# Recurrent mixer heads: key factors as a logarithm in the exponents, once per head

## The chip, the core and the metric

The kernel runs on one core of a Trainium2 chip. The metric is the device time of one execution in microseconds (us): the median of several runs. TensorE multiplies matrices, VectorE, ScalarE and GpSimd do the elementwise work, SyncE issues most DMAs. Each engine works through its own queue in order.

## What is computed

Two transformer blocks on 512 tokens of width 1024, all in float32. The second block has a mixer with two kinds of heads, and the change is in the first kind: four recurrent heads of 128 channels (HGRN2), computed in chunks. In the reference, with q, f, k, v per head:

```python
f = lbf + (1.0 - lbf) * jax.nn.sigmoid(f_logit)
k = 1.0 - f
bc = jnp.cumsum(to_chunks(jnp.log(f)), axis=3)
decay = jnp.exp(jnp.where(causal, bt[t] - bt[s], -jnp.inf))
a = jnp.einsum('bhtd,bhsd,bhtsd->bhts', qt, kt, decay)      # within a chunk
o = einsum(a, v) + (q * exp(bt)) @ state                    # and from the chunks before
```

So the weight of key s for query t is the sum over channels of q[t] k[s] exp(b[t] - b[s]), where b is the running sum of log f. The second kind are eight stick-breaking heads. The results of both, normed and joined, go through `w_out`. Around the mixers stand three feed-forward parts, the first block's attention, a memory cross attention and the norms.

## The kernel before

Every dense product is made of three passes over split operands (a high and a low part): `mm3`, lines 372 to 374. `split` (L403 on ScalarE, L404 on VectorE) makes the parts. TensorE's order is written by the program. In the mixers `weave` makes it: a planner takes chains (heads) and fills (slabs of weights against all tokens), with a model of each step's cost on VectorE ("D"), ScalarE ("A") and GpSimd ("G"). While no step of a chain is due by that model, it takes the next piece of the fills. At most three chains are active (`WIDTH`). The other engines' queues are ordered by a list scheduler that knows the dependencies and its own estimates, and that also hands out the 16 buffers of the ring "w" (`wt()`).

A recurrent head is the chain `hgrn_chain`. L1388 makes kf = 1 - f on ScalarE, L1389 log f, L1391 the running sum b on VectorE (a scan that restarts at every chunk of 64). The causal weights are then made in levels. Level 0 is the diagonal (L1460, kf against q). For the half lengths 64, 32, 16, 8, 4, 2, 1 the tokens are taken in pairs of a lower and an upper half, and for 128 and 256 over whole chunks. For each of these nine levels `exponents` or `far_exponents` fills a buffer e of 128x512: its lower halves with ref - b, its upper halves with b - ref, on GpSimd (L1417 and L1419, or L1448 and L1450). `decayed` takes the exponential on ScalarE (L1404 and L1405 for 64, L1407 for the others), multiplies the lower halves by kf (L1408) and the upper ones by q (L1409), both on VectorE. `scores` then multiplies lower by upper on TensorE (L1468 up to 64, L1481 and L1487 beyond), and L1470 puts the product into place. The exponents are prepared `LOOK` + 1 = 3 levels ahead of the scores. `prepared` (L1501 to L1505) and `first` (L1507) tell the planner what a level and a head's beginning cost.

Other lines that the text names: a stick-breaking head (`sb_head`) masks (L1556, L1559), takes an exponential and a logarithm (L1560, L1561), scans (L1564), subtracts (L1566), takes an exponential (L1567) and is transposed on TensorE (the flips, L756). The head norm is L1365 to L1367, with L1588 (`sb_tail`) or L1533 (`hgrn_tail`) behind it. `fill_part` splits finished mixer outputs into the buffers "h" and multiplies them by slabs of `w_out`, which L1631 adds up.

Of the kernel before, what the change touches and what calls it, by code (L numbers as in the profile page):

```python
# [14 lines left out]
AF = mybir.ActivationFunctionType  # L15
ALU = mybir.AluOpType
# [4 lines left out]
D = 1024  # L21
# [57 lines left out]
def STEP(pe=0.0, dve=0.0, act=0.0, ops=(), lat=0.0, free=0, need=0, back=0):  # L79

    return Step(pe, dve, act, ops, lat, free, need, back)
# [11 lines left out]
def transformer_blocks_kernel(  # L95
# [41 lines left out]
    V, A, G, T = nc.vector, nc.scalar, nc.gpsimd, nc.tensor  # L137
# [13 lines left out]
    def big(tag, bufs, dt=F32, cols=512):  # L151
        return sp.tile([P, cols], dt, tag=tag, bufs=bufs, name=nm(tag))
# [10 lines left out]
    def wt(dt=F32):  # L163
        return big("w", WBUFS, dt)
# [4 lines left out]
    def aux():  # L169
        return pb.tile([P, 512], F32, tag="b", name=nm("b"))  # L170

    def col(n=4, bufs=20):
        return sp.tile([P, n], F32, tag=f"c{n}", bufs=bufs, name=nm("c"))
# [1061 lines left out]
    tiny, eps6 = small[:, 0:1], small[:, 1:2]  # L1235
# [148 lines left out]
    def hgrn_chain(hd):  # L1384
        q, f = store["q", hd], store["f", hd]
        yield STEP()
        kf = wt()
        A.activation(kf, f, AF.Copy, scale=-1.0, bias=1.0)  # L1388
        A.activation(f, f, AF.Ln, bias=tiny)  # L1389
        b = f  # L1390
        V.tensor_tensor_scan(out=b, data0=reset, data1=f, initial=0.0, op0=ALU.mult, op1=ALU.add)  # L1391

        bc = b.rearrange("p (c t) -> p c t", t=64)
        tot = bc[:, :, 63]

        def halves(t, hl):
            v = t.rearrange("p (b u c) -> p b u c", u=2, c=hl)
            return v[:, :, 0, :], v[:, :, 1, :]

        def decayed(e, hl):  # L1400

            el, eu = halves(e, hl)
            if hl == 64:
                A.activation(el, el, AF.Exp)  # L1404
                A.activation(eu, halves(b, hl)[1], AF.Exp)  # L1405
            else:
                A.activation(e, e, AF.Exp)  # L1407
            V.tensor_tensor(el, el, halves(kf, hl)[0], op=ALU.mult)  # L1408
            V.tensor_tensor(eu, eu, halves(q, hl)[1], op=ALU.mult)  # L1409

        def exponents(hl):
            e = wt()
            el, eu = halves(e, hl)
            bl, bu = halves(b, hl)
            nb = 256 // hl
            ref = bl[:, :, hl - 1:hl].to_broadcast([P, nb, hl])
            G.tensor_tensor(el, ref, bl, op=ALU.subtract)  # L1417
            if hl != 64:
                G.tensor_tensor(eu, bu, ref, op=ALU.subtract)  # L1419
            decayed(e, hl)  # L1420
            return e

        ad = wt()

        w0, w13, w2 = [wt(F32R) for b in range(2)], [wt(F32R) for b in range(2)], wt(F32R)
        w2 = [w2[:, :256], w2[:, 256:]]

        def diagonals(t):
            return t.rearrange("p (a c) -> p a c", c=P)[:, 0:4:3]

        def far_exponents(hl):
            nch = hl // 64
            nb = 256 // hl
            lowc, upc = col(8), col(8)
            tv = tot.rearrange("p (b u c) -> p b u c", u=2, c=nch)
            lv = lowc[:, :4].rearrange("p (b c) -> p b c", c=nch)
            uv = upc[:, :4].rearrange("p (b c) -> p b c", c=nch)
            G.tensor_copy(lv[:, :, nch - 1], tv[:, :, 0, nch - 1])
            G.memset(uv[:, :, 0:1], 0.0)
            for c in range(nch - 1):  # L1440
                G.tensor_tensor(lv[:, :, nch - 2 - c], lv[:, :, nch - 1 - c],
                                tv[:, :, 0, nch - 2 - c], op=ALU.add)
                G.tensor_tensor(uv[:, :, c + 1], uv[:, :, c], tv[:, :, 1, c], op=ALU.add)
            e = wt()
            ev = e.rearrange("p (b u c t) -> p b u c t", u=2, c=nch, t=64)
            bv = b.rearrange("p (b u c t) -> p b u c t", u=2, c=nch, t=64)
            for bb in range(nb):
                G.tensor_tensor(ev[:, bb, 0], lv[:, bb].unsqueeze(2).to_broadcast([P, nch, 64]),  # L1448
                                bv[:, bb, 0], op=ALU.subtract)
                G.tensor_tensor(ev[:, bb, 1], uv[:, bb].unsqueeze(2).to_broadcast([P, nch, 64]),  # L1450
                                bv[:, bb, 1], op=ALU.add)
            decayed(e, hl)
            return e

        def scores(hl, e):
            ps = aux()
            if hl == 0:
                for gg in range(4):
                    sl = slice(gg * P, (gg + 1) * P)
                    T.matmul(ps[:, sl], kf[:, sl], q[:, sl], start=True, stop=True)  # L1460
                V.tensor_tensor(ad.rearrange("p (g t) -> p g t", g=4),
                                ps.rearrange("p (g t) -> p g t", g=4),
                                ident.unsqueeze(1).to_broadcast([P, 4, P]), op=ALU.mult)
                return 0.43
            if hl <= 64:
                for gg in range(4):
                    up = e[:, gg * P:(gg + 1) * P].rearrange("p (b u c) -> p b u c", u=2, c=hl)[:, :, 1, :]
                    T.matmul(ps[:, gg * 64:(gg + 1) * 64], e[:, gg * P:(gg + 1) * P], up,  # L1468
                             start=True, stop=True)
                V.copy_predicated(  # L1470
                    halves(ad, hl)[1],
                    masks[hl].rearrange("p (b c) -> p b c", c=hl),
                    ps[:, :256].rearrange("p (b c) -> p b c", c=hl))
                if hl == 1:
                    split(w0[0][:, :P], w0[1][:, :P], ad[:, :P])
                    split(*[diagonals(t) for t in w13], ad.rearrange("p (a c) -> p a c", c=P)[:, 1:4:2])
                    split(w2[0][:, :P], w2[1][:, :P], ad[:, 256:256 + P])
                return 0.21
            if hl == 128:
                for bb in range(2):  # L1480
                    T.matmul(ps[:, bb * P:(bb + 1) * P], e[:, bb * 256:bb * 256 + P],  # L1481
                             e[:, bb * 256 + P:bb * 256 + 256], start=True, stop=True)
                for bb, t in enumerate((w0, w2)):
                    split(t[0][:, P:256], t[1][:, P:256], ps[:, bb * P:(bb + 1) * P])
            else:
                for bb in range(2):
                    T.matmul(ps[:, bb * 256:(bb + 1) * 256], e[:, bb * P:(bb + 1) * P],  # L1487
                             e[:, 256:512], start=True, stop=True)
                split(w0[0][:, 256:], w0[1][:, 256:], ps[:, :256])
                split(w13[0][:, P:384], w13[1][:, P:384], ps[:, 256:])  # L1490
            return 0.22 if hl == 128 else 0.86

        order = (0, 64) + LEVELS + (128, 256)
        es = {0: None}

        def prepare(n):
            if n < len(order):
                hl = order[n]
                es[hl] = far_exponents(hl) if hl > 64 else exponents(hl)

        def prepared(n):  # L1501
            if n >= len(order):
                return ()
            far = order[n] > 64
            return (("G", 2.3),) * far + (("G", 0.7), ("G", 0.7)) * (not far) + (("A", 0.55), ("D", 0.7))  # L1505

        first = (("A", 0.6), ("A", 0.6), ("D", 0.6))  # L1507
        for n in range(1, LOOK + 1):
            prepare(n)
            first += prepared(n)  # L1510
        yield STEP(ops=(first,), lat=TLAT[2], need=1)
        for n, hl in enumerate(order):
            prepare(n + LOOK + 1)
            pe = scores(hl, es.pop(hl))
            after = {0: (("D", 0.6),), 1: (("D", 0.35), ("A", 0.7), ("D", 0.75)), 128: (("A", 0.32), ("D", 0.4)),
                     256: (("A", 0.55), ("D", 0.7))}.get(hl, (("D", 0.35),))
            last = n == len(order) - 1
            yield STEP(pe=pe, ops=(after, prepared(n + LOOK + 1)), lat=HLAT, need=int(not last), free=1,
                       back=0 if last else HBACK)
        store["w", hd] = w0, [t[:, :384] for t in w13], w2, [t[:, 384:] for t in w13]  # L1520
# [352 lines left out]
```

## Time and profile before

| | |
|---|---|
| median of 3 runs | 1912.51 us (1911.18 to 1912.85) |
| profiled execution | 1912.74 us, of which the span from first to last instruction is 1911.0 us |
| TensorE busy | 1881.5 us (98%) |
| VectorE busy | 1388.6 us (73%) |
| ScalarE busy | 929.8 us (49%) |
| GpSimd busy | 174.9 us (9%) |
| mixers of the second block | about 1180 to 1430 us; recurrent heads 0 and 1 from 1213, heads 2 and 3 from 1331 us |

All shares are of the span. Matmuls overlap in the pipeline, so that a busy TensorE is one that always has an instruction under way; its granted clock is given apart, as a share of 2.4 GHz. Idle time of an engine is put down to the instruction that released it last ("<-"). Idle time of an engine other than the bound costs nothing by itself.

### The profile page before, as it was taken

The page shows a single profiled execution, that of the slowest core. Times are in us where ns is not written, and L with a number is a line of the kernel's source. Part 1 is how long each engine was busy: PE and PEld are TensorE (multiplying, and loading weights), DVE is VectorE, ACT ScalarE, POOL GpSimd, SP SyncE. Part 2 cuts the span into 40 slices and gives each one's busy share as a digit, 9 for nine tenths or more (in the row PEclk, how much of TensorE's full clock was granted, in tenths as well). Part 3 has the DMA queues.
Part 4 walks back from the last instruction along what each step waited for, and adds up shares of the span by engine and source line. Part 5 has one row for each costly group of instructions (what it writes and reads, how often), then busy time and mean ns, then how long its engine had stood idle before and what let it go on. Part 6 is the DMA issues. An engine that isn't in the chain of part 4 may idle for free.

```text
span 1911.0 us, 29337 instructions
## 1 busy us (share of the span) xinstructions
PE 1881.5 (98%) x11566; PEld 1688.3 (88%) x11566; DVE 1388.6 (73%) x2217; ACT 929.8 (49%) x1537; POOL 174.9 (9%) x272
## 2 busy tenths in 40 slices
PE   8999999999999999999999999999999999999998
PEld 6899888888999998899999988888888778999997
DVE  6777635468878786777877757888976448878785
ACT  5666534364544445443434356657565344344443
POOL 2330100060000002000000010430410000000000
PEclk9999999999999999999999999999999999999999
DMA  5212224452233324423232342121343222232322
GB/s 180 67 55 68 78 66 154 166 176 89 89 111 96 120 93 162 143 67 111 90 119 99 114 160 71 63 94 39 103 152 133 77 85 82 99 111 89 111 88 89
DMA packets 164908, 198.69 MB, mean 104 GB/s; under 512 B 7745, under 2 KB 131746, under 8 KB 164770
## 3 DMA queue, kind: packets, MB, share of 16 engines
q1 hardware_dynamic: 163202, 192.10, 30.8%
q0 software_dynamic: 1280, 4.20, 0.6%
q8 instruction: 91, 1.49, 0.3%
q10 hardware_dynamic: 288, 0.52, 0.1%
q14 instruction: 47, 0.39, 0.1%
HBM read 186.30 MB, written 10.49 MB: 103 GB/s over the span
## 4 chain that ended last, share of the span: by engine, by line
PE 87%; issue 5%; DVE 3%; ACT 2%; POOL 1%; DMA 1%; SPq 0%; POOLq 0%; DVEq 0%; ACTq 0%
PE b L372 15%; PE b L374 15%; PE b L373 15%; PE a L372 11%; PE a L374 11%; PE a L373 11%; PE a L514 4%; PE b L616 1%; DVE wl L404 1%; PE b L490 1%; PE b L756 1%; PE b L1468 1%; PE b L1774 1%; DMA q<-mact_d 0%; PE b L886 0%
## 5 line engine op out<-in xcount | busy, mean ns | idle before, releaser
L404 DVE TENSOR_TENSOR wl<-wr,wh 128x1024 fp32r<-128x1024 f32 (+1 forms) x381 | 463.0, 1218 | 272.9 <-ACT wh L403 266.4
L403 ACT CAST wh<-wr 128x1024 fp32r<-128x1024 f32 (+1 forms) x381 | 394.1, 1036 | 443.9 <-PE b L373 144.1
L372 PE MATMUL b<-wh,q 128*128 128x512 f32 x672 | 262.4, 390 | 0.0
L373 PE MATMUL b<-wl,q 128*128 128x512 f32 x672 | 262.0, 390 | 0.0
L374 PE MATMUL b<-wh,q 128*128 128x512 f32 x664 | 258.2, 389 | 0.0
L372 PE MATMUL a<-h,wh 128*128 128x512 f32 (+1 forms) x660 | 238.4, 361 | 0.0
L374 PE MATMUL a<-h,wl 128*128 128x512 f32 (+1 forms) x660 | 234.9, 356 | 0.0
L373 PE MATMUL a<-h,wh 128*128 128x512 f32 (+1 forms) x660 | 234.7, 356 | 0.0
L373 PE MATMUL b<-h,wh 128*128 128x256 f32 (+1 forms) x568 | 175.9, 310 | 0.0
L372 PE MATMUL b<-h,wh 128*128 128x256 f32 (+1 forms) x568 | 175.9, 310 | 0.0
L374 PE MATMUL b<-h,wl 128*128 128x256 f32 (+1 forms) x568 | 175.9, 310 | 0.0
L374 PEld LDWEIGHTS b<-wh,q 128*128 128x128 f32 x664 | 124.6, 188 | 26.6
L372 PEld LDWEIGHTS b<-wh,q 128*128 128x128 f32 x672 | 126.3, 188 | 24.6
L373 PEld LDWEIGHTS b<-wl,q 128*128 128x128 f32 x672 | 126.3, 188 | 24.3
L373 PE MATMUL a<-s,wh 128*128 128x256 f32 (+1 forms) x488 | 141.2, 289 | 0.0
L374 PEld LDWEIGHTS a<-h,wl 128*128 128x128 f32 x660 | 124.6, 189 | 18.3
L372 PEld LDWEIGHTS a<-h,wh 128*128 128x128 f32 x660 | 124.7, 189 | 17.9 <-issue 0.5
L373 PEld LDWEIGHTS a<-h,wh 128*128 128x128 f32 x660 | 124.7, 189 | 17.8 <-issue 0.5
L373 PEld LDWEIGHTS b<-h,wh 128*128 128x128 f32 x568 | 108.3, 191 | 5.6
L374 PEld LDWEIGHTS b<-h,wl 128*128 128x128 f32 x568 | 108.2, 191 | 5.6
L372 PEld LDWEIGHTS b<-h,wh 128*128 128x128 f32 x568 | 108.1, 190 | 5.6
L374 PE MATMUL a<-wh,h 128*128 128x256 f32 x368 | 106.6, 290 | 4.5 <-DVE h L404 4.5
(379 smaller groups left out, 4179.7 us busy)
## 6 DMA issues: line engine op xcount, KB each, us to landing
wr<-in_ffn_w_gu_dram SPq DMA_DIRECT2D x88, 512.0 KB
wr<-in_w_in_dram SPq DMA_DIRECT2D x68, 512.0 KB
wr<-in_ffn_w_down_dram SPq DMA_DIRECT2D x44, 512.0 KB
wr<-in_w_gate_dram SPq DMA_DIRECT2D x22, 512.0 KB
wr<-in_w_up_dram SPq DMA_DIRECT2D x22, 512.0 KB
wr<-in_w_down_dram SPq DMA_DIRECT2D x22, 512.0 KB
wr<-in_mem_w_kv_dram SPq DMA_DIRECT2D x16, 512.0 KB
wr<-in_w_out_dram SPq DMA_DIRECT2D x10, 512.0 KB
```

The costliest lines, as they stand in the source:

```text
L372: T.matmul(ps, lh, rh, start=first, stop=False)
L373: T.matmul(ps, lh, rl, start=False, stop=False)
L374: T.matmul(ps, ll, rh, start=False, stop=last)
L403: A.copy(hi, src)
L404: V.tensor_tensor(lo, src, f32(hi), op=ALU.subtract)
L490: T.transpose(banks[k][:, t * P:(t + 1) * P], self.s[t, k // 4][:, (k % 4) * P:(k % 4 + 1) * P], ident)
L514: T.matmul(accs[m], lh, rh, start=c == 0 and n in (0, 2), stop=c == KT - 1 and n > 3)
L616: T.matmul(ps, lh[n], rh[n], start=n == 0, stop=n == 1)
L756: T.transpose(ps[:, o * P:(o + 1) * P], blk, ident)
L1468: T.matmul(ps[:, gg * 64:(gg + 1) * 64], e[:, gg * P:(gg + 1) * P], up, start=True, stop=True)
L1774: T.matmul(po, lh, rh, start=n == 0, stop=n == 5)
```

## The change

Once per head the logarithm of kf is taken (ScalarE, with the same small bias of 1e-30 as log f) and subtracted from b: bk = b - log kf. At each of the nine levels the lower exponents are ref - bk instead of ref - b, so that their exponential already holds the factor kf, and the multiplication of the lower halves goes away. Level 0 still multiplies by kf. The planner's costs are changed with it.

```diff
         V.tensor_tensor_scan(out=b, data0=reset, data1=f, initial=0.0, op0=ALU.mult, op1=ALU.add)
+        bk = wt()
+        A.activation(bk, kf, AF.Ln, bias=tiny)
+        V.tensor_tensor(bk, b, bk, op=ALU.subtract)
...
-            V.tensor_tensor(el, el, halves(kf, hl)[0], op=ALU.mult)
             V.tensor_tensor(eu, eu, halves(q, hl)[1], op=ALU.mult)
...
-            G.tensor_tensor(el, ref, bl, op=ALU.subtract)
+            G.tensor_tensor(el, ref, halves(bk, hl)[0], op=ALU.subtract)
...
-            bv = b.rearrange("p (b u c t) -> p b u c t", u=2, c=nch, t=64)
+            bv, bkv = [t.rearrange("p (b u c t) -> p b u c t", u=2, c=nch, t=64) for t in (b, bk)]
             for bb in range(nb):
                 G.tensor_tensor(ev[:, bb, 0], lv[:, bb].unsqueeze(2).to_broadcast([P, nch, 64]),
-                                bv[:, bb, 0], op=ALU.subtract)
+                                bkv[:, bb, 0], op=ALU.subtract)
...
-            return (("G", 2.3),) * far + (("G", 0.7), ("G", 0.7)) * (not far) + (("A", 0.55), ("D", 0.7))
-        first = (("A", 0.6), ("A", 0.6), ("D", 0.6))
+            return (("G", 2.3),) * far + (("G", 0.7), ("G", 0.7)) * (not far) + (("A", 0.55), ("D", 0.5))
+        first = (("A", 0.6), ("A", 0.6), ("D", 1.2), ("A", 0.6), ("D", 0.7))
```

## Rows read from the trace of the kernel before

**Rows 1.** The page: span, then busy us (share) xinstructions of each engine.

```profile
span 1911.0 us, 29337 instructions
...
PE 1881.5 (98%) x11566; PEld 1688.3 (88%) x11566; DVE 1388.6 (73%) x2217; ACT 929.8 (49%) x1537; POOL 174.9 (9%) x272
```

**Rows 2.** Waits of PE, 1180 to 1460 us: total us, times, longest us.

```profile
PE a L374 <- DVE h L404: 4.5, 4, 1.9
PE b L756 <- ACT w L1567: 2.1, 2, 1.4
...
PE b L756 <- DVE w L1470: 0.3, 1, 0.3
```

**Rows 3.** Stretches: length, then busy (x) of PE, PEld, DVE, ACT, POOL, PEclk, DMA.

```profile
1216.00:1262.00 46.00, 44.30 (x325) 41.22 (x323) 41.04 (x72) 26.49 (x50) 33.53 (x62) 1.00 0.14 46
1334.00:1396.00 62.00, 58.07 (x449) 55.95 (x449) 54.49 (x108) 33.80 (x67) 31.19 (x62) 0.94 0.33 104
```

**Rows 4.** Timeline of PE: start us, us, instruction, [idle before <-releaser].

```profile
1236.94 0.66 PE L756 MATMUL b<-ident,w 128*128 128x128 f32 x4 [1.38 <-ACT w L1567]
...
1346.35 0.58 PE L374 MATMUL a<-wh,h 128*128 128x256 f32 x1 [1.92 <-DVE h L404]
...
1399.37 0.39 PE L374 MATMUL a<-wh,h 128*128 128x256 f32 x1 [0.84 <-DVE h L404]
```

**Rows 5.** The stretch of the lower granted clock, columns as in rows 3.

```profile
1345.09:1351.92 6.83, 5.57 (x26) 5.57 (x27) 5.94 (x9) 3.22 (x8) 2.33 (x4) 0.50 0.94 322
```

**Rows 6.** Groups, 1200 to 1420 us: busy us, mean ns | idle before <-releasers.

```profile
L1408 DVE TENSOR_TENSOR w<-w,w 128x256 f32<-128x256 f32 x36 | 19.2, 534 | 8.8 <-ACT w L1407 7.1 <-ACT w L1404 1.4
...
L404 DVE TENSOR_TENSOR h<-y,h 128x512 fp32r<-128x512 f32 x6 | 4.1, 698 | 0.0
...
L1389 ACT ACTIVATE q<-q,small 128x512 f32<-128x512 f32 x4 | 2.9, 714 | 0.0
```

**Rows 7.** Timeline of DVE and ACT ahead of the wait at 1236.94 us.

```profile
1230.81 0.78 DVE L1408 TENSOR_TENSOR w<-w,w 128x256 f32<-128x256 f32 x1 [0.89 <-ACT w L1407]
...
1233.95 0.77 DVE L1408 TENSOR_TENSOR w<-w,w 128x256 f32<-128x256 f32 x1
1234.64 1.13 DVE L1566 TENSOR_TENSOR w<-w,w 128x512 f32<-128x512 f32 x1
...
1235.26 0.63 ACT L1407 ACTIVATE w<-w 128x512 f32<-128x512 f32 x1 [1.65 <-POOL w L1419]
...
1236.27 0.62 ACT L1567 ACTIVATE w<-w 128x512 f32<-128x512 f32 x1
```

**Rows 8.** Timeline of DVE, POOL and ACT, head 2's start to the h splits.

```profile
1333.03 1.22 DVE L1391 TENSOR_TENSOR_SCAN q<-reset,q 128x512 f32<-128x512 f32 x1
...
1334.38 1.37 POOL L1417 TENSOR_TENSOR w<-q 128x256 f32<-128x256 f32 x2 [72.28 <-PE b L1365]
...
1336.55 0.63 ACT L1407 ACTIVATE w<-w 128x512 f32<-128x512 f32 x1 [1.10 <-POOL w L1419]
...
1337.22 0.44 DVE L1408 TENSOR_TENSOR w<-w,w 128x256 f32<-128x256 f32 x1 [0.98 <-ACT w L1407]
...
1339.68 1.12 ACT L403 CAST h<-y 128x512 fp32r<-128x512 f32 x2
```

**Rows 9.** Timeline of DVE and PE around head 1's first level product.

```profile
1225.34 0.85 DVE L1409 TENSOR_TENSOR w<-w,q 128x256 f32<-128x256 f32 x1
...
1230.05 1.00 PE L1468 MATMUL b<-w 128*128 128x64 f32 x8
...
1235.08 0.49 PE L756 MATMUL b<-ident,w 128*128 128x128 f32 x3
```

**Rows 10.** Timeline of POOL and DVE: small additions beside a scan.

```profile
1220.50 0.18 POOL L1443 TENSOR_TENSOR c<-c,q 128x2 f32<-128x2 f32 x1
...
1221.43 1.22 DVE L1391 TENSOR_TENSOR_SCAN q<-reset,q 128x512 f32<-128x512 f32 x1
1221.51 1.11 POOL L1443 TENSOR_TENSOR c<-c,q 128x1 f32<-128x1 f32 x1
```

## The prediction

> **What bounds the kernel now.** I read the busy table first: TensorE works 1881.5 of 1911.0 us, VectorE 1388.6, ScalarE 929.8, GpSimd 174.9 [rows 1]. TensorE is the bound, in program order, so an edit that touches no matmul can only give back time in which TensorE waits or runs at half clock. The second view is the list of TensorE's waits in the stretch from 1180 to 1460 us, which holds the second block's mixers. Three lines matter: 4.5 us in 4 waits for the VectorE half of a split into h (L404), 2.1 us in 2 waits for the exponential L1567 of a stick-breaking head, 0.3 us for L1470 [rows 2]. No line there is a wait of L1468 for its exponents: the products that the change feeds are never late. The third view, by stretches, shows VectorE at 41.04 of 46 us while heads 0 and 1 run and at 54.49 of 62 us while heads 2 and 3 do [rows 3]. VectorE is nearly full there, but it isn't what the span waits for.
>
> The fourth view is TensorE's timeline at its waits [rows 4]. There are three places.
> (a) At 1236.94 the flips L756 wait 1.38 us for L1567; with the 0.3 of [rows 2] that is about 1.7 us.
> (b) From 1340 to 1346.4 the first w_out slab waits for the splits of its operands: 4.5 of [rows 2] less the 0.84 of (c), about 3.7 us, the last wait being 1.92. Here the clock falls: the granted clock is 0.50 (1.2 instead of 2.4 GHz) for 6.83 us, with TensorE busy in 5.57 of them [rows 5]. At full clock that work would have taken half, so the fall costs about 2.8 us and place (b) 6.5.
> (c) At 1399.37 the same kind of split keeps TensorE 0.84 us.
> Together 9.0 us. This is the ceiling of any gain: 0.47% of the span.
>
> **The change part by part.** The multiplication L1408 goes away 36 times at a mean of 534 ns: 19.2 us of VectorE [rows 6]. Added on VectorE are four subtractions of 128x512 from SBUF, which the trace doesn't show in this form. The nearest row is the split of the same shape with both inputs in SBUF, 698 ns [rows 6]; no reason lets them cost nothing, and by the spread of L1408 (its mean of 534 against single ones of 0.78 in [rows 7]) one may take half as much again, so 2.8 to 4.2 us; I take 2.8, as most of L1408's instructions are near the short end. VectorE's work falls by 16.4 us (15.0 to 16.4). ScalarE gets four logarithms of 128x512, each like L1389's 714 ns [rows 6]: 2.9 us. GpSimd keeps the same subtractions with another operand. So the work falls on an engine that is not the bound, and only what it does at (a), (b) and (c) counts.
>
> Head start. The first lower subtraction of a head now waits for the scan, then for the new subtraction: 0.70 us later; the logarithm itself runs on ScalarE beside the scan, which takes 1.22 us [rows 8]. What hides the 0.70: head 1's first exponents are done at 1225.34 plus 0.85, and TensorE takes them at 1230.05 [rows 9], 3.9 us later. Zero on the path, 0.70 less the cover if that were gone.
>
> Place (a). On VectorE two L1408, at 1230.81 and 1233.95, stand ahead of the subtraction L1566 at 1234.64 on which L1567 waits: 0.78 + 0.77 us. But L1567 stands in ScalarE's queue behind the exponential L1407 at 1235.26, which had waited 1.65 us for GpSimd [rows 7]. If that order stays, nothing is gained, and the head start's 0.7 may come through GpSimd on top. If the scheduler, which now sees L1566 ready earlier, puts L1567 first, L1566 ends about 1.55 us earlier and the wait is nearly gone. Bounds -1.7 to +0.7; I take -1.2, for the two removed instructions lie directly ahead. The Trainium skill, "SBUF — State Buffer", on engine-side ports, says that the pair of ports shared by VectorE and GpSimd is an exclusive lock when a VectorE instruction has two SBUF inputs, held for the whole instruction. The trace agrees: a GpSimd addition of a single column took 1.11 us while the scan of 1.22 us ran, and one of two columns 0.18 just before it [rows 10]. L1408 has two SBUF inputs, so by that rule GpSimd would also get on sooner, L1407 would wait less, and (a) would be worth its whole -1.7: the sum below would be 0.5 us lower.
>
> Place (b). The h splits begin on ScalarE at 1339.68, behind the norm logarithm L1366, which stands behind L1407 at 1336.55, which had waited 1.10 us for GpSimd, which began head 2's exponents at 1334.38, after the scan of 1333.03 [rows 8]. This is the head start without cover: the new subtraction comes between scan and GpSimd, and everything behind shifts by 0.70 us, the splits included. Two L1408 leave VectorE there, but it was idle before the second (0.98 us, for L1407), so they give nothing back [rows 8]. Bounds -6.5 (a new order of work ends the wait and the fall of the clock) to +0.7; I take +0.7, the order of before.
>
> Place (c). The late split follows the norm of a finished mixer output; L1408 is not its releaser. Bounds -0.84 to 0; I take -0.2.
>
> Planner and buffers. L1505 now reckons 0.5 instead of 0.7 us of VectorE a level, and L1507 adds 0.6 to the scan and two operations, 0.6 and 0.7, with their hops: a head's first product is planned some 1.8 us later (1.9 + 0.3 - 0.4). The order of TensorE's work in the stage is thus made anew. It adds no work, and fills take the place of what moves back, so I take zero; its ends are the rivals'. The buffer bk is new, but kf, held to the last level before, is now free after the level 0 product; only between the two does a head hold one more of the 16 w buffers. I take zero.
>
> Sum: -1.2 + 0.7 - 0.2 = -0.7 us against the profiled execution's 1912.74 us (a span of 1911.0 and 1.7 around it). That execution lies 0.2 above the median of 1912.51, so I predict 1911.8 us. A difference of under 0.2% (3.8 us) is about what a measurement of this kernel can't tell from no change.
>
> **Rivals.** First, the gain is real: the new order and the emptier VectorE queue end the wait at (b). Then the clock doesn't fall either: -6.5 there and -1.2 at (a), about 1904.8. For it: all of (b) depends on where the first slab stands against ScalarE's and VectorE's queues, and both move. Against: the slab begins as soon as the fills ahead of it end, and the change touches no fill.
> Second, slower, by one mechanism: the planner moves a head's first products behind the flips at 1235.08, because they are due 1.8 us later. The flips then come earlier than L1567, while its end, held by GpSimd, doesn't move. Ahead of them stand 40 products of heads 0 and 1, and eight take 1.00 us [rows 9], so 5.0 us; added to the 1.7 of (a) the wait passes the 3.7 us that was followed by half clock at (b), and a fall like that of [rows 5] adds 2.8: +7.8, about 1920. It decides only once the planned delay exceeds the 5.0 us from head 1's product at 1230.05 to the flips [rows 9]; two heads delayed by 1.8 each reach 3.6. So it is possible, not likely. A new wait like (b) at any other slab would cost the same 6.5.
> Third, VectorE's relief doesn't appear, because the instructions that are left wait longer for GpSimd and the subtractions cost their upper bound. As TensorE is the bound, the time would still be within 1 us of before, 1913.
>
> **How the numbers follow.** The forecast, between 1908.7 and 1916.3, has 0.49, and the third rival 0.05 beside it on the same side of the bound; faster (the first rival, or parts of it that pass 3.8 us) 0.28; slower (the second, or a wait like (b) elsewhere) 0.18. So faster 0.28, same 0.54, slower 0.18. The range for 8 in 10 starts at the ceiling, 1912.5 - 9.0 = 1903.5, and ends short of the second rival's full price, at 1918.
>
> **What would show it.** Right: VectorE's busy time lower by about 16 us with the span within 4; no L1408 multiplication, no new wait of L1468; (b) still there with its stretch at 0.50, a little longer. Wrong: no fall of the clock near the first w_out slab (first rival), a second stretch at 0.50 in the mixers or a flip that waits over 3 us (second), or a wait of the level products for the new chain, which would say that the head start isn't covered. If time changes outside 1216 to 1410 us, the scheduler moved more than I reckon with.

## The result

The changed kernel takes 1927.15 us (median of 6 runs) against 1911.59 for the kernel before (6 runs): a ratio of 1.0082, 95% interval 1.0072 to 1.0092. It is 15.6 us slower: 9 us above the range of the forecast, which ended at 1918, and not the small gain that was expected.

In the changed kernel the new logarithm is L1395 and its subtraction L1396. The exponentials are L1409, L1410 and L1412, the upper multiplication L1413, GpSimd's subtractions L1421 and L1423, its column operations for the far levels L1442 to L1447 (copies, fills and additions of one or two columns). Every later line of the kernel before stands four lines further down. The page, as in [rows 1]:

```profile
span 1925.4 us, 29320 instructions
...
PE 1882.6 (98%) x11566; PEld 1688.4 (88%) x11566; DVE 1373.8 (71%) x2185; ACT 933.1 (48%) x1541; POOL 172.7 (9%) x272
```

VectorE works 14.8 us less (15.0 to 16.4 were forecast). The span is 14.4 us longer all the same. The waits of TensorE in the mixers (total us, times, longest), which answer to [rows 2], say where:

```profile
PE a L372 <- ACT h L403: 10.9, 3, 4.0
PE a L372 <- DVE q L404: 5.3, 1, 5.3
PE b L1485 <- DVE w L1413: 1.9, 1, 1.9
PE a L374 <- DVE h L404: 1.9, 1, 1.9
PE b L1365 <- ACT w L1588: 0.8, 2, 0.6
PE b L756 <- ACT w L1571: 0.7, 1, 0.7
```

All waits of TensorE there are 21.7 us, with one of 0.2 not shown; before they were 8.0. That is 13.7 of the 14.4 us. Two places carry it: the splits into h at the first w_out slab, place (b), now 12.7 us (10.9 + 1.9) instead of 3.9, and a new one, a wait of 5.3 us for the split that empties a fill's bank, which I call (d). The flips of place (a) no longer wait, and the wait at (c) is gone. A wait of 1.9 us of the level 128 product L1485 is new. The clock, as in [rows 5] (stretch, length, busy time of PE, PEld, DVE, ACT, POOL, granted clock, DMA):

```profile
1230.68:1234.09 3.41, 2.83 (x7) 2.25 (x8) 2.14 (x6) 2.15 (x4) 1.34 (x2) 0.50 0.01 2
1346.73:1363.80 17.07, 6.67 (x23) 5.33 (x24) 9.16 (x15) 9.14 (x18) 5.20 (x16) 0.50 0.46 154
```

Both places bring half clock. TensorE has 9.5 us of work in these two stretches, half of which is lost, 4.8 us instead of the 2.8 of before. Waits and clock together are 15.7 us more, 1.3 over what the span grew.

What the bank of (d) waits for stands in the timelines of GpSimd, ScalarE, VectorE and TensorE (start, us, instruction, idle before):

```profile
1222.28 1.23 DVE L1391 TENSOR_TENSOR_SCAN q<-reset,q 128x512 f32<-128x512 f32 x1 [0.19 <-ACT q L1389]
...
1223.57 1.10 POOL L1442 COPY c<-q 128x2 f32<-128x2 f32 x1 [2.60 <-DVE q L1391]
...
1227.60 1.20 POOL L1421 TENSOR_TENSOR w<-q,w 128x256 f32<-128x256 f32 x2
...
1228.25 0.42 ACT L1409 ACTIVATE w<-w 128x256 f32<-128x256 f32 x1 [2.91 <-POOL w L1421]
1229.42 0.63 ACT L1412 ACTIVATE w<-w 128x512 f32<-128x512 f32 x1 [0.76 <-POOL w L1423]
1229.95 0.36 ACT L403 CAST q<-a 128x256 fp32r<-128x256 f32 x1
...
1230.79 0.41 DVE L404 TENSOR_TENSOR q<-a,q 128x256 fp32r<-128x256 f32 x1
...
1231.26 0.79 PE L372 MATMUL a<-h,wh 128*128 128x512 f32 x1 [5.30 <-DVE q L404]
```

Head 1's lower subtraction has to wait for bk, so the list scheduler gave the gap to the column operations, which need b alone. GpSimd runs all twelve first and comes to L1421 at 1227.60, 4.1 us after the scan (in [rows 8] the same subtraction of head 2 began 0.1 us after it). ScalarE stands at L1409 and L1412 for 3.7 us, and behind them in its queue waits the copy that empties the bank. So there was one suspect, GpSimd's queue, and one rival: the new order of TensorE's work, which the planner made from its new numbers.

### The profile page after: what moved, and what is told of

Same layout as the page of the kernel before. It is cut to its first block, busy times and chain, and to the rows that moved or that the text cites. A ratio compares the mean times of both kernels' runs of the same rounds, so it can differ in the third digit from the quotient of the medians.

```text
span 1925.4 us, 29320 instructions
## 1 busy us (share of the span) xinstructions
PE 1882.6 (98%) x11566; PEld 1688.4 (88%) x11566; DVE 1373.8 (71%) x2185; ACT 933.1 (48%) x1541; POOL 172.7 (9%) x272
## 5 line engine op out<-in xcount | busy, mean ns | idle before, releaser
L374 PEld LDWEIGHTS a<-h,wl 128*128 128x128 f32 x660 | 124.8, 189 | 18.4
L372 PE MATMUL a<-wh,h 128*128 128x256 f32 x368 | 108.7, 295 | 10.9 <-ACT h L403 10.9
```

The costliest lines, as they stand in the source:

```text
L372: T.matmul(ps, lh, rh, start=first, stop=False)
L374: T.matmul(ps, ll, rh, start=False, stop=last)
```

## The experiments

Each was run against the kernel before, which took 1911.3 to 1911.4 us (medians of 13 to 25 runs). TensorE's order of work is that of before in the runs with the old planner numbers, and that of the changed kernel in the runs with both new ones, instruction by instruction.

The first two rows are those of the result above. The last two columns are those of the profiled execution, from 1180 to 1460 us: all waits of TensorE that the view lists, added up, and the length of the stretches at a granted clock of 0.50, with TensorE's busy time in them. Half of that busy time is an estimate of what the clock costs.

| run | TensorE's order | us | ratio to before, 95% | waits, us | half clock, us (busy) |
|---|---|---|---|---|---|
| the kernel before | before | 1911.6 | | 8.0 | 6.8 (5.6) |
| the change | changed | 1927.15 | 1.0082 (1.0072 to 1.0092) | 21.7 | 20.5 (9.5) |
| e1 planner numbers only | changed | 1918.3 | 1.0037 (1.0024 to 1.0050) | 12.2 | 20.5 (16.1) |
| e2 change with old planner numbers | before | 1911.35 | 0.9999 (0.9990 to 1.0009) | 8.9 | 6.8 (4.8) |
| e3 columns behind | changed | 1923.7 | 1.0062 (1.0045 to 1.0079) | 17.3 | 20.5 (11.4) |
| e4 levels 64 and 32 as before | changed | 1921.7 | 1.0056 (1.0041 to 1.0071) | 18.4 | 13.7 (7.0) |
| e5 level number only | a third | 1920.9 | 1.0052 (1.0037 to 1.0067) | 14.1 | 13.7 (11.0) |
| e6 beginning's number only | a fourth | 1929.0 | 1.0092 (1.0077 to 1.0107) | 18.6 | 27.3 (21.5) |
| e7 splits first | changed | 1919.2 | 1.0040 (1.0025 to 1.0055) | 13.1 | 13.7 (11.7) |
| e8 e2, columns behind, splits first | before | 1910.8 | 0.9999 (0.9989 to 1.0008) | 8.6 | 3.4 (2.9) |
| e9 heads 2 and 3 as before | changed | 1923.1 | 1.0067 (1.0050 to 1.0084) | 15.6 | 20.5 (13.8) |
| e10 before, splits first | before | 1910.0 | 0.9998 (0.9988 to 1.0007) | 7.2 | 6.8 (6.1) |
| e11 columns behind, splits first | changed | 1915.6 | 1.0021 (1.0012 to 1.0030) | 10.0 | 10.2 (9.1) |
| e12 e8 and stick-breaking steps first | before | 1909.9 | 0.9997 (0.9987 to 1.0006) | 8.0 | 3.4 (3.4) |

In all fourteen profiled executions the span less the waits less half of that busy time is 1897 to 1901 us, while the spans lie between 1908 and 1929. So these two columns hold nearly all of what the profiled executions differ by. The executions of one kernel lie up to 5 us apart, and the profiled one needn't be the middle one.

**e1, the planner's numbers alone**, on the kernel before:

```diff
-            return (... + (("A", 0.55), ("D", 0.7))
-        first = (("A", 0.6), ("A", 0.6), ("D", 0.6))
+            return (... + (("A", 0.55), ("D", 0.5))
+        first = (("A", 0.6), ("A", 0.6), ("D", 1.2), ("A", 0.6), ("D", 0.7))
```

> The kernel before with the change's planner costs alone: the multiplications stay, there is no bk, TensorE's order is that of the changed kernel. Theory (GpSimd's column additions for the far levels, which now run ahead of a head's first lower exponents, hold ScalarE's queue): about 1912 us, within 3 of before, since the columns stay behind the first exponents. Rival (the new order of TensorE's work makes the waits): 1924 to 1928 us, with the 5.3 us wait for the split at about 1226 us and the 17 us of half clock at the first w_out slab. Were it only the latency of the new logarithm and subtraction, the time would be that of the theory too.

**e2, the change with the planner's old numbers**: the reverse of e1's diff, on the changed kernel.

> The changed kernel with the planner costs of before: TensorE's order is that of before, the columns run first on GpSimd. Theory (columns first): 1920 to 1930 us, with ScalarE's first exponential of a head waiting some 2 us or more for GpSimd at each of the four heads. Rival (order of TensorE's work): 1909 to 1914 us.

e1 took 1918.3 us and e2 1911.35. My theory fell on both: with the columns first but the old order the change costs nothing that can be measured, and the new order costs 6.9 us without any bk. Yet e1 also stays 6 us short of the rival's range, so the new order alone isn't the whole either. Of the 15.6 us, 6.9 are the order's, none the arithmetic's, and some 9 come only when both are there. The same lines as above in e2 show how:

```profile
1227.60 1.21 POOL L1421 TENSOR_TENSOR w<-q,w 128x256 f32<-128x256 f32 x2
...
1228.25 0.42 ACT L1409 ACTIVATE w<-w 128x256 f32<-128x256 f32 x1 [2.91 <-POOL w L1421]
...
1230.81 0.41 DVE L404 TENSOR_TENSOR q<-a,q 128x256 fp32r<-128x256 f32 x1
```

The elementwise queues do the same things at the same times, to 0.02 us; the bank is empty at 1231.2 in both. But the waits of TensorE in e2 are these:

```profile
PE a L374 <- DVE h L404: 3.5, 4, 1.5
PE b L756 <- ACT w L1571: 2.2, 3, 1.3
PE a L372 <- ACT h L403: 1.5, 1, 1.5
PE a L372 <- DVE q L404: 0.9, 1, 0.9
```

The wait for the bank is 0.9 instead of 5.3 us. In the old order 40 products of heads 0 and 1 (the last eight in [rows 9]) stand ahead of the piece of the fill that needs the bank; in the new order they come after it, and TensorE meets the bank 4.4 us sooner. In e1 the same place waits 2.1 us, because there the bank is emptied sooner:

```profile
PE a L372 <- ACT h L403: 3.7, 2, 2.0
PE a L374 <- DVE h L404: 2.6, 3, 1.1
PE b L1481 <- DVE w L1409: 2.3, 1, 2.3
PE a L372 <- DVE q L404: 2.1, 1, 2.1
```

So each half of the change takes away cover for the other. The order brings the fills forward, the arithmetic makes the queues that serve them later. The same holds at (b): 3.9 us before, 4.8 in e2 (the 5.0 of h above less 0.2 at (c)), 6.3 in e1, 12.7 with both. The 2.3 us of L1481 come from the order alone. Head 2 shows how near the order brings things: its scan begins 7.1 us before TensorE gets to the slab in the kernel before, and 2.7 us before in e1 and in the changed kernel.

In e1 the clock costs more, by that estimate, than the added waits. Its stretches at half clock, with columns as above, are these:

```profile
1227.19:1230.60 3.41, 3.41 (x10) 2.86 (x11) 1.93 (x4) 2.26 (x4) 3.41 (x8) 0.50 0.89 296
1343.24:1356.89 13.65, 9.46 (x37) 8.29 (x38) 10.26 (x18) 6.97 (x14) 4.51 (x16) 0.50 0.59 192
1401.27:1404.68 3.41, 3.19 (x9) 2.52 (x10) 2.10 (x8) 1.56 (x5) 0.00 (x0) 0.50 0.00 0
```

Each begins in a wait or within 0.1 us of its end (the bank, the slab, L1481). Half of the 16.1 us of work is 8.0 us, 5.2 more than before, while the waits grew by 4.2. The changed kernel has 9.5 us more of waits than e1 but loses 3.3 us less to the clock, as TensorE had less to do in its slow stretches.

**e3, the columns behind.** The changed kernel, with the column operations ordered on GpSimd behind the first two levels' exponents. `behind`, whose definition is left out here, adds an order on GpSimd only, behind the level 32 instruction L1423. Lines of this kernel stand seven further down than those of the changed one:

```diff
-            G.tensor_copy(lv[:, :, nch - 1], tv[:, :, 0, nch - 1])
-            G.memset(uv[:, :, 0:1], 0.0)
+            behind(G.tensor_copy(lv[:, :, nch - 1], tv[:, :, 0, nch - 1]))
+            behind(G.memset(uv[:, :, 0:1], 0.0))
```

> The changed kernel, where the column operations of the far levels are ordered behind the first two levels' exponents on GpSimd; the order of TensorE, ScalarE and VectorE is that of the changed kernel. Theory (columns first): 1910 to 1917 us; the first subtraction begins about 0.7 us after the scan instead of 2.2 to 4.1, and the 5.3 us wait and most of the half clock go. Rivals (TensorE's order, or the latency of logarithm and subtraction): still 1923 to 1928 us.

**e4, the first two levels as before**, bk from level 16 on:

```diff
+            if hl in (64, 32):
+                V.tensor_tensor(el, el, halves(kf, hl)[0], op=ALU.mult)
...
-            G.tensor_tensor(el, ref, halves(bk, hl)[0], op=ALU.subtract)
+            G.tensor_tensor(el, ref, bl if hl in (64, 32) else halves(bk, hl)[0], op=ALU.subtract)
```

> The changed kernel, but levels 64 and 32, those that stand at a head's beginning, take b and multiply by kf as before; bk is used from level 16 on. TensorE's order is that of the changed kernel, the columns go behind by themselves, and no wait for bk stands at the beginning. Theory (columns first): 1909 to 1914 us. Rival (TensorE's order): 1923 to 1928 us. If the latency of logarithm and subtraction matters beside the order on GpSimd, this is faster than the run with the columns set behind; if not, the two are equal within 1 us.

e3 took 1923.7 us, in the rivals' range, and e4 1921.7, 1.3 below it. What GpSimd's order does is real but small: in e3 the wait for the bank falls from 5.3 to 2.8 us and (b) from 12.7 to 10.9, together with 3.5 us of time. In e4 the two levels at a head's beginning don't wait for bk, and yet (b) has 11.0 us of waits (5.9 and 5.1 below), against 6.3 in e1. So at (b) the change costs something beside that wait. In e4, as in the changed kernel, the slab's last splits stand behind head 3's exponentials on ScalarE; in e1 they stand ahead of them. That the logarithm and the subtraction put them there, by their time in the queues, is likely but not shown.

```profile
PE a L372 <- ACT h L403: 5.9, 2, 3.5
PE a L374 <- DVE h L404: 5.1, 3, 3.7
```

**e5 and e6, one planner number each**, both on the changed kernel: the new D of a level with the old `first`, and the old D with the new `first`.

> The changed kernel with only one of its planner numbers: a level costs 0.5 instead of 0.7 us of VectorE, a head's beginning is reckoned as before. TensorE's order is a third one, different from both kernels'. Theory (a head's longer planned beginning moves its first products back, and the fills that come in their place find their bank or operands not ready): 1909 to 1915 us, as with all of the old numbers. Rival (any new order costs, the level number as much): 1918 us or more.

> The changed kernel with the other planner number alone: the longer beginning of a head, a level reckoned at 0.7 as before. TensorE's order is a fourth one. Theory (the planned beginning moves the fills forward): 1921 to 1928 us, with the wait for the split of a fill near 1230 us and over 9 us of waits at the first w_out slab. Rival (the level number or their sum makes it): under 1916 us.

e5 went the rival's way: 1920.9 us. e6 took 1929.0 us, 1 us above the theory's range, and not for the theory's reason: the wait for the bank is there, but (b) has 4.0 us instead of over 9. Each number makes an order of its own. e5 waits 3.7 us for flips, 2.6 for the bank and 4.4 at (b); e6 waits 3.6, 5.3 and 4.0, and 4.7 for level products, which waited nowhere in the kernel before. e6 has fewer waits than the change and is slower, since its four stretches at half clock hold 21.5 us of work instead of 9.5. No one number is to blame. Whichever of the three new orders is taken, the kernel with it is 7 to 18 us slower than before (e1, the change, e5, e6). e5 and e6 hold bk too; what their orders cost without it was not run. What makes the order of before better than these three, in a form that one could write into the planner, these runs don't show.

**e7, the splits first.** The changed kernel; the splits of finished mixer outputs get priority in the other engines' queues, and TensorE's order stays:

```diff
-                for k in ks:
-                    msp[k] = halves_of(mixed[k], None, "h")
+                with tc.high_priority(CPRIO):
+                    for k in ks:
+                        msp[k] = halves_of(mixed[k], None, "h")
```

> The changed kernel with the order of TensorE untouched, but the splits of finished mixer outputs (fill_part) are given priority in the other engines' queues, so that they should stand ahead of a recurrent head's beginning. Theory (the loss at the first w_out slab is ScalarE's and VectorE's queue: its splits behind the exponentials of heads 2 and 3, which wait for GpSimd): the 12.7 us of waits there fall to under 5 and most of the 17 us of half clock goes: 1912 to 1918 us; the 5.3 us wait at 1231 us stays. Rival (the splits are late because their buffers or inputs are): 1924 to 1928 us.

1919.2 us, 8.0 less than the change, 1.2 over the range expected. (b) falls from 12.7 to 4.2 us of waits; what is left is this:

```profile
PE a L372 <- DVE q L404: 5.3, 1, 5.3
PE a L372 <- ACT h L403: 3.9, 1, 3.9
...
PE a L374 <- DVE h L404: 0.3, 1, 0.3
```

The first split still stands behind the exponentials of head 2, and the wait of 5.3 us for the bank stays. So most of (b)'s waits were a place in a queue. In the changed kernel's ScalarE queue one sees it (before, head 2's L1407 came at 1336.55, ahead of the splits [rows 8]):

```profile
1345.89 0.42 ACT L1409 ACTIVATE w<-w 128x256 f32<-128x256 f32 x1 [1.90 <-POOL w L1421]
1347.07 0.63 ACT L1412 ACTIVATE w<-w 128x512 f32<-128x512 f32 x1 [0.76 <-POOL w L1423]
1347.60 0.60 ACT L403 CAST h<-y 128x512 fp32r<-128x512 f32 x1
...
1358.09 0.42 ACT L1409 ACTIVATE w<-w 128x256 f32<-128x256 f32 x1 [2.86 <-POOL w L1421]
1359.26 0.63 ACT L1412 ACTIVATE w<-w 128x512 f32<-128x512 f32 x1 [0.76 <-POOL w L1423]
1359.80 0.60 ACT L403 CAST h<-y 128x512 fp32r<-128x512 f32 x1
```

Head 2's exponentials stand right ahead of the slab's first split and head 3's ahead of its last, since in the new order the slab comes sooner after head 2's start.

The half clock, most of which was expected to go in e7, stayed: its stretch at the slab is shorter, 10.2 instead of 17.1 us, but TensorE has more work in it, 8.5 instead of 6.7 us.

**e9, heads 2 and 3 as before**: `if hd < 2` around bk and `if hd > 1` around the multiplication by kf, TensorE's order that of the change.

> The changed kernel, but heads 2 and 3 take b and multiply by kf as before; heads 0 and 1 keep bk. TensorE's order is that of the changed kernel. Theory (what the new order costs grows with the bk chain where a head's beginning meets a fill that waits): the 5.3 us wait at 1231 us stays, the first w_out slab falls from 12.7 us of waits to the 6.3 of the run with the planner alone: 1919 to 1923 us. Rival (bk costs by itself, wherever it stands, through ScalarE's logarithm and the buffer it holds): half of what lies between that run and the changed kernel is left at each pair of heads, and the slab keeps 9 us or more: over 1923 us.

```profile
PE a L372 <- DVE q L404: 5.3, 1, 5.3
PE a L372 <- ACT h L403: 3.7, 2, 2.0
PE a L374 <- DVE h L404: 2.6, 3, 1.1
```

(b) is back at the 6.3 us of e1, while the 5.3 at heads 0 and 1 stays: the cost lies where a head's beginning meets a fill. The time, 1923.1 us, is 0.1 above the line between the two expectations and 4.8 above e1. The profiled executions, e9's fastest and e1's slowest, are only 1.9 us apart; between them the longer wait for the bank adds 3.2 us, and the clock takes 1.2 less. What the other executions of e9 add isn't shown.

**e11, both queue orders put right** (e3 and e7 together):

> The changed kernel with both queue orders put right: the columns of the far levels behind the first exponents on GpSimd, and the splits of finished mixer outputs with priority. TensorE's order is untouched. Theory: the two effects add, 1919.2 less the 3.5 us of the columns: 1914 to 1917 us, with some 2.8 us of wait left at 1229 us and 1.9 at 1402. Rival (they are one effect seen twice): 1918 to 1920 us.

1915.6 us, as expected: the two effects, 3.5 and 8.0 us, add to 11.5. What remains is 2.7 us for the bank, 3.1 at (b), 1.9 for L1492, the level 128 product (L1485 of the change), and 10.2 us at half clock with 9.1 us of work.

**e8, e10 and e12, in the old order.** e8 is e2 with the orders of e3 and e7. e10 is the kernel before with e7's priority. e12 is e8 with `tc.high_priority(CPRIO)` around L1560 to L1571 of the stick-breaking heads.

> The changed arithmetic with the planner numbers of before, the column operations behind the first exponents on GpSimd and the splits of finished mixer outputs with priority. Theory: the wait at the first w_out slab (4.8 us and 6.8 us of half clock with the old numbers) shrinks to under 2 us and the clock stays up there, the 0.9 us wait for the split at 1231 us goes: 1904 to 1909 us, less than both kernels. Rival (the slab's wait is one for buffers or for the mixer outputs, not for queues): 1909 to 1913 us.

> The kernel before with priority for the splits of finished mixer outputs, nothing else: the control to the two runs that give them priority with the new arithmetic. Theory: the slab's wait of 3.7 us and its half clock shrink, 1907 to 1911 us. If the priority alone reaches the time of the changed arithmetic with it (1910.8), the arithmetic is worth nothing there either.

> The changed arithmetic, the planner numbers of before, columns behind, splits with priority, and the elementwise steps of the stick-breaking heads with priority too, so that their last exponential doesn't stand behind those of the recurrent heads. Theory (queues): the 2.1 us wait of the flips at 1236 us goes, 1906 to 1910 us. Rival: other work comes later by as much, and the time stays at 1910 to 1913 us.

1910.8, 1910.0 and 1909.9 us: none can be told from the kernel before. e8 went the rival's way: (b) fell from 4.8 to 3.2 us with a new 1.4 us wait behind it. e12 hit its time, but not for its reason: the wait of the flips didn't go, it grew to 3.3 us. e10 reaches e8's time without bk. So with priority too, the arithmetic is worth nothing that can be measured here, and none of these versions beats the kernel before clearly. In e10 (b) fell from 3.9 to 3.1 us of waits, but its half clock stayed.

## Why the prediction was wrong

**The bound and the ceiling.** Right. TensorE is the bound, VectorE's 16 us aren't on its path, and e2, the arithmetic by itself, is at 1911.35 us where the sum said 1911.8. That this agrees so well is partly luck: (a) gained 0.3 us and not 1.2, (c) 0.6 and not 0.2, and the wait of 0.9 us for the bank wasn't in the sum. The new subtraction took 684 ns (698 assumed), the logarithm 715 (714 assumed).

**Head start.** Two errors, of which only the second one mattered. The subtraction on GpSimd came not 0.70 us later but 2.2 to 4.1 us after the scan, because the scheduler filled the gap with the column operations. In e3, without them in the way, it came 0.9 us after head 0's scan and 1.8 after head 1's, whose new subtraction stood behind a weight split in VectorE's queue. I looked for cover only at the products that the change feeds, and these indeed never waited in the old order. But ScalarE's queue is in order, and what stood behind the waiting exponentials was the emptying of a fill's bank. I did follow that queue at (b) and stopped there.

**Place (b).** +0.7 us was taken. In the old order it is +0.8 (e2), so the step holds there. With the new order it was 8.8 us of waits: the term was right for a position that the planner then moved.

**Places (a) and (c).** -1.2 us at (a) was wrong: in e2, in the old order, the flips wait 1.34 us as before (1.38), since their exponential stayed behind those of the recurrent heads, as the other bound had it. The wait at (c) fell to 0.22 us in e2.

**Planner and buffers.** This is the step that failed. I set it at zero, "fills take the place of what moves back". They do; but a fill needs a bank and operands, and these come from the same queues. e1 puts a price of 6.9 us on the planner's numbers alone, in waits and in half clock, and 8.9 more come from their meeting with the new arithmetic. The second rival had the kind of mechanism, a new order that runs ahead of its producers, at the flips, where it didn't come; its last sentence, a new wait like (b) at another slab, was nearer. All that was slower had a chance of 0.18, which was too small. I treated a plan made anew as neutral, though the trace of before shows that the stage's waits all hang on a few us of distance between a step and its producer.

**What was said would show it.** A second stretch at half clock in the mixers was named as the mark of the slower case, and it is there.

## What to carry to other kernels

A change of arithmetic and a change of a planner's numbers are two changes: run each alone first. Here the one was worth nothing that could be measured, the other cost 7 us, and together they cost 16, since each took away the distance that covered the other. When an operation gets a new input, ask what the in-order queue of each engine behind it holds, and what the scheduler will put into the gap, not only who uses the result.

## What the runs showed of the hardware

Small GpSimd operations aren't free. Additions of one column and of two took the same 0.18 to 0.19 us undisturbed, against 0.6 for 128x256, so that a dozen column operations, with no VectorE scan beside them, held GpSimd for 2.1 us (1217.06 to 1219.16) ahead of work that was waited for.

```profile
1217.06 0.19 POOL L1442 COPY c<-q 128x2 f32<-128x2 f32 x1 [94.73 <-DVE q L1391]
...
1219.16 1.21 POOL L1421 TENSOR_TENSOR w<-q,w 128x256 f32<-128x256 f32 x2
```

In the changed kernel four waits of TensorE close together (3.87, 3.95, 1.87 and 3.05 us) go with 17.07 us at half clock, in which it worked 6.67 us; there the waits cost more than the clock (12.7 us against 3.3). It isn't always so: at the same slab e1 has 6.3 us of waits and loses 4.7 us to the clock. What a slow stretch costs goes by the work that falls into it.
